# Mixer: the recurrent branch's two gates as products of 64 rows per head

## The chip, the cores and the metric
One Trainium2 chip, one of its cores. The metric is the time of one execution of the whole kernel on the device, in microseconds (us); lower is better. TensorE's clock has two levels, 1.2 and 2.4 GHz, and the trace records which was granted (1.00 is 2.4 GHz, 0.50 is 1.2 GHz).

## The reference
One layer over 2048 positions of width 1024: a mixer of three branches (A: gMLP, B: recurrent, C: S5), an output product, a mixture of experts, a final norm. The change lies in branch B, 6 heads of 64 columns:

```python
xc = causal_depthwise_conv(x_raw, conv_w, conv_b)
xh = xc.reshape(bsz, seq, B_HEADS, HEAD_DIM)
r = sigmoid(einsum("bshi,hij->bshj", xh, rg_w).reshape(bsz, seq, width) + rg_b)
i = sigmoid(einsum("bshi,hij->bshj", xh, ig_w).reshape(bsz, seq, width) + ig_b)
log_a = -LRU_C * r * softplus(-lam)
a = exp(log_a);  b = sqrt(-expm1(2.0 * log_a)) * (i * xc)
h = linear_recurrence(a, b)
return h * gelu(g_raw)
```

Each head has its own 64 x 64 matrix for the gate r and another for the gate i.

## The kernel before, in words
Everything up to the router is in `phases12`. Columns of the mixer lie on partitions: a "column chunk" `i` (0 to 2) of branch B is 128 partitions, two heads of 64. Positions are done in two halves `h` of 1024; a half in two quarters `q` of 512 positions. So `b_z(h, i, w, q)` and the generator `b_post(h, i, q, ...)` run 12 times; each of these runs is called a step here, step 1 to step 12 in the order of the program.

`b_z` issues 2 x 24 products on TensorE (PE) for the two column groups x and g of a chunk (`split3`, L90 to L92, the tile `z`). `b_post` then does: the convolution (ACT L904, DVE L171 on `bxc`), the gelu of g (ACT L914), the two gates (L920 and L921), a chain of ACT operations with two loads of ACT's function tables (L925 to L928), DVE operations and the scan (L934), and the product with the gelu; later its square (ACT L941) and the sums over channels (PE L945).

The gates are the place of the change. For each gate `j` a block-diagonal 128 x 128 matrix `bd[:, j, i, :]` (two heads' 64 x 64 blocks, zeros elsewhere; zeroed once by POOL at L434, filled by four DMAs at L438) is multiplied with `xc`, 128 partitions by 512 positions, and ACT takes the tanh of the product out of PSUM, 128 x 512 at a time, into `btr` (gate r) or `bti` (gate i):

```python
            for j, o in enumerate((tr, ti)):
                ps = bank(psm, "m")
                T.matmul(ps, bd[:, j, i, :], xc, start=True, stop=True)
                A.activation(o, ps, AF.Tanh, scale=0.5, bias=b_cols[:, i, 1 + j:2 + j])
```

In float32 a product is issued to the array as two passes, each with its own load of weights; a step's two products are four passes.

What sets the order: each engine does its instructions in the order in which they were written. The steps, the preparation of the S5 constants (`s5_consts`, `angles`), the S5 batches (`c_batch`), the next weights (`wgen`: ACT L212 and DVE L171 on `w`, which split a weight into a high and a low part) and branch A's later part (`part`) are generators that a ticker (`Flow`) advances between PE's products. A table (`TURNS`) moves some of their turns. The change doesn't touch it, and no generator's turn moves.

PSUM: the products of the gates, the constants' small products (L732), the S5 products (L796 into `u`, L815 to L817 into `y`), the sums (L945) and some transposes (L235) share the pool `psm` of two banks, taken in turn. An instruction that writes a bank waits until the last reader of the use before has read it. So in the kernel before the next user after a step takes the bank of gate r and waits for ACT's first tanh of the step; the one after that takes the bank of gate i and waits for ACT's second.

Of the kernel before, what the change touches and what calls it, by code (L numbers as in the profile page):

```python
# [9 lines left out]
F32 = mybir.dt.float32  # L10
# [3 lines left out]
AF = mybir.ActivationFunctionType  # L14
# [5 lines left out]
P = 128  # L20
# [124 lines left out]
def phases12(tc, io, hd, hc, tab, gcol, ident, c8, stg):  # L145


    nc = tc.nc
    V, A, G, T = nc.vector, nc.scalar, nc.gpsimd, nc.tensor
    ctx = ExitStack()  # L150
    with ctx:
# [4 lines left out]
        base = pool("base")  # L156
# [6 lines left out]
        psm = pool("psm", 2, space=PSUM)  # L163
        drp = pool("dr", space=DRAM)
        yTd = drp.tile([16, P, 8, P], F32, name="yTd")
        bank = lambda p, nm: p.tile([P, 512], F32, name=nm, tag="b")
# [201 lines left out]
        F.add(wg)  # L368

        gv = base.tile([P, 384], F32, name="gv")  # L370
        bd = base.tile([P, 2, 3, P], F32, name="bd")
        wsT = base.tile([P, 6, P], F32, name="wsT")
        glu = base.tile([P, 2, 256], F32, name="glu")
        glb = base.tile([P, 2], F32, name="glb")
# [8 lines left out]
        b_cols = base.tile([P, 3, 4], F32, name="b_cols")  # L383
# [7 lines left out]
        def s5_consts(pp):  # L391
# [39 lines left out]
            yield 0  # L431
            V.memset(hst, 0.0)
            yield 0
            G.memset(bd, 0.0)  # L434
            for j, nm in enumerate(("b_rg_w", "b_ig_w")):
                for h in range(2):
                    src = io[nm][0].rearrange("(i h) a b -> h a i b", h=2)[h]
                    nc.sync.dma_start(out=bd[h * 64:(h + 1) * 64, j, :, h * 64:(h + 1) * 64], in_=src)  # L438
            nc.sync.dma_start(out=gv, in_=io["a_v_norm_g"][0:1, :].to_broadcast((P, 384)))
            yield 0  # L440
            nc.sync.dma_start(out=glu, in_=io["c_glu_w"][0].rearrange("(k p) n -> p k n", p=P))
# [1 line left out]
            ps = bank(pst, "tp")  # L443
# [8 lines left out]
            ps = bank(pst, "tp")  # L452
# [154 lines left out]
            for j in range(2):  # L607
                ps = bank(pst, "tp")
# [88 lines left out]
            for g in range(0, 16, 4):  # L697
                dst = lambda slot: cstP[:, slot, g:g + 4, :]

                i = g // 4 % 2  # L700
# [14 lines left out]
                m = ms[1][:, :, 1:9, :].rearrange("p g s c -> p g (s c)")  # L715
                ps = bank(pst, "tp").rearrange("p (a b) -> p a b", b=P)
                for j in range(4):
                    T.transpose(ps[:, j, :], us[0][:, j].rearrange("p s c -> p (s c)"), ident)
                o = big[2 * i + 1].rearrange("p (a b) -> p a b", b=P)
# [10 lines left out]
                ps = bank(psm, "tp").rearrange("p (a b) -> p a b", b=P)  # L730
# [13 lines left out]
            for h in range(2):  # L744
                ps = bank(pst, "tp").rearrange("p (h j) -> p h j", j=P)
# [153 lines left out]
        def b_post(h, i, q, px, st):  # L899
# [15 lines left out]
            yield  # L915
            tr = bw.tile([P, N], F32, name="btr")
            ti = bw.tile([P, N], F32, name="bti")
            for j, o in enumerate((tr, ti)):
                ps = bank(psm, "m")
                T.matmul(ps, bd[:, j, i, :], xc, start=True, stop=True)  # L920
                A.activation(o, ps, AF.Tanh, scale=0.5, bias=b_cols[:, i, 1 + j:2 + j])  # L921
            yield

            sq = bw.tile([P, N], F32, name="bsq")
# [18 lines left out]
            ps = bank(psm, "m")  # L943
# [1053 lines left out]
```

## Time and profile before

| | us |
|---|---|
| median of 3 runs | 1603.42 (1600.23 to 1604.23) |
| the profiled execution's own time | 1600.41 |
| its span, first to last instruction | 1598.6 |
| mean granted clock | 0.963 |
| PE, ACT, DVE busy | 1492.4, 864.5, 986.4 |
| first product of the gates in steps 1 to 6, at | 99.3, 115.3, 132.8, 154.2, 178.5, 205.8 |
| the same in steps 7 to 12, at | 317.8, 341.5, 355.0, 371.3, 423.9, 448.6 |

The mixer takes about the first 700 us, routing and experts the rest; branch B's steps lie between 99 and 453 us. In the rows below, engines are PE (TensorE's products), PEld (its weight loads), ACT (ScalarE), DVE (VectorE), POOL (GpSimd) and SP (the queue that issues most DMAs). A line such as L921 is a line of the kernel before. A row of a timeline is: start, duration, engine, line, operation, output tile and input tiles, shape, count of merged instructions, and in brackets how long the engine had been idle before and what ended that. Products overlap their neighbours at their ends, so the end of a product in a timeline is later than the moment at which the next one may stream; the chain of waits cuts them to where the next began.

### The profile page before, as it was taken

The page shows a single profiled execution, that of the slowest core. Times are in us where ns is not written, and L with a number is a line of the kernel's source. Part 1 is how long each engine was busy: PE and PEld are TensorE (multiplying, and loading weights), DVE is VectorE, ACT ScalarE, POOL GpSimd, SP SyncE. Part 2 cuts the span into 40 slices and gives each one's busy share as a digit, 9 for nine tenths or more (in the row PEclk, how much of TensorE's full clock was granted, in tenths as well). Part 3 has the DMA queues.
Part 4 walks back from the last instruction along what each step waited for, and adds up shares of the span by engine and source line. Part 5 has one row for each costly group of instructions (what it writes and reads, how often), then busy time and mean ns, then how long its engine had stood idle before and what let it go on. Part 6 is the DMA issues. An engine that isn't in the chain of part 4 may idle for free.

```text
span 1598.6 us, 25576 instructions
## 1 busy us (share of the span) xinstructions
PE 1492.4 (93%) x8373; PEld 1286.7 (80%) x8374; DVE 986.4 (62%) x2011; ACT 864.5 (54%) x1913; POOL 471.1 (29%) x396
## 2 busy tenths in 40 slices
PE   7998879999999999997799899999999999999993
PEld 6866678878899989997588678888888888888882
DVE  6588661674543487887879886668888857303001
ACT  6377543677544534312346546666566665666662
POOL 0132000000000000010355436555555555445442
PEclk9999888999999999998799899999999999999997
DMA  6247632313532726707577887679888877534342
GB/s 179 66 92 139 188 113 76 123 53 105 166 106 73 264 80 233 281 28 265 200 226 233 248 254 202 201 209 278 269 234 230 250 218 209 139 71 111 89 111 77
DMA packets 213774, 267.46 MB, mean 167 GB/s; under 512 B 34824, under 2 KB 178384, under 8 KB 213648
## 3 DMA queue, kind: packets, MB, share of 16 engines
q1 hardware_dynamic: 187808, 201.95, 39.9%
q0 software_dynamic: 24480, 62.27, 16.1%
q10 hardware_dynamic: 1360, 1.57, 0.3%
q8 instruction: 78, 1.28, 0.3%
q14 instruction: 48, 0.39, 0.1%
HBM read 217.09 MB, written 76.94 MB: 184 GB/s over the span
## 4 chain that ended last, share of the span: by engine, by line
PE 74%; DVE 13%; DMA 5%; ACT 4%; issue 2%; SPq 1%; POOL 0%; POOLq 0%; ACTq 0%; DVEq 0%
PE pg L1688 23%; PE z L90 8%; PE z L92 8%; PE z L91 8%; PE pd L1729 4%; PE pd L1728 4%; PE pd L1727 4%; DMA stg<-in_expert_w_up_dram 2%; DVE ring L1614 2%; DVE ring L1596 2%; PE pt L1695 2%; DVE w L171 1%; PE m L920 1%; PE pt L1700 1%; PE ph L1695 1%
## 5 line engine op out<-in xcount | busy, mean ns | idle before, releaser
L1688 PE MATMUL pg<-ring,xs 128*128 x2016 | 487.3, 394 | 11.8 <-DVE ring L1614 10.6
L1688 PEld LDWEIGHTS pg<-ring,xs 128*128 128x128 f32 x2016 | 378.1, 189 | 91.6 <-issue 14.0
L90 PE MATMUL z<-w,xT 128*128 128x256 f32 (+1 forms) x848 | 250.2, 295 | 4.5 <-DVE ht L171 3.2
L92 PE MATMUL z<-w,xT 128*128 128x256 f32 (+1 forms) x848 | 244.3, 288 | 7.2 <-DVE xT L169 7.2
L91 PE MATMUL z<-w,xT 128*128 128x256 f32 (+1 forms) x848 | 244.3, 288 | 0.0
L1596 DVE TENSOR_SCALAR ring<-stg,gcol 128x512 fp32r<-128x512 f32 x242 | 128.5, 592 | 164.8 <-PE pg L1688 86.2
L1614 DVE SCALAR_TENSOR_TENSOR ring<-stg,gcol,ring 128x512 fp32r<-128x512 f32 x248 | 222.2, 956 | 0.0
L92 PEld LDWEIGHTS z<-w,xT 128*128 128x128 f32 x848 | 163.8, 193 | 8.5 <-DVE xT L169 8.5
L90 PEld LDWEIGHTS z<-w,xT 128*128 128x128 f32 x848 | 164.2, 194 | 7.7 <-issue 4.2
L91 PEld LDWEIGHTS z<-w,xT 128*128 128x128 f32 x848 | 164.4, 194 | 1.4 <-issue 1.4
L1727 PE MATMUL pd<-ring,hh 128*128 x336 | 132.1, 393 | 1.7 <-DVE hh L1633 1.7
L1728 PE MATMUL pd<-ring,hh 128*128 x336 | 131.7, 392 | 0.0
L1729 PE MATMUL pd<-ring,hh 128*128 x336 | 131.7, 392 | 0.0
L1892 POOL DMA_INDIRECT hd<-yb,tab x41 | 76.9, 1874 | 182.5 <-ACT yb L1831 182.5
L171 DVE SCALAR_TENSOR_TENSOR w<-raw,vec,w 128x256 fp32r<-128x256 f32 x176 | 82.0, 511 | 61.9 <-ACT w L212 61.8
L1941 POOL TENSOR_TENSOR yb<-yb,gf 128x1024 f32<-128x1024 f32 x40 | 116.9, 2923 | 2.5 <-ACT hu L1856 2.5
L1906 POOL TENSOR_TENSOR hs<-hs,hu 128x256 f32<-128x256 f32 x84 | 99.8, 1188 | 54.4 <-ACT hu L1810 53.7
L90 PE MATMUL z<-xT,w 128*128 128x512 f32 x256 | 110.5, 432 | 0.2 <-ACT xT L298 0.2
L212 ACT ACTIVATE w<-raw,vec 128x256 fp32r<-128x256 f32 x176 | 77.2, 497 | 59.9 <-PE z L92 36.5
L171 DVE SCALAR_TENSOR_TENSOR ht<-z,rsd,ht 128x256 f32<-128x256 f32 x176 | 85.1, 484 | 29.2 <-PE z L92 21.3
L91 PE MATMUL z<-xT,w 128*128 128x512 f32 x256 | 102.2, 399 | 0.2 <-DVE xT L169 0.2
L92 PE MATMUL z<-xT,w 128*128 128x512 f32 x256 | 102.0, 398 | 0.0
(440 smaller groups left out, 2576.7 us busy)
## 6 DMA issues: line engine op xcount, KB each, us to landing
stg<-in_expert_w_gate_dram SPq DMA_DIRECT2D x62, 512.0 KB, 4.3
stg<-in_expert_w_up_dram SPq DMA_DIRECT2D x62, 512.0 KB, 5.8
stg<-in_expert_w_down_dram SPq DMA_DIRECT2D x60, 512.0 KB, 4.5
raw<-in_w_in_dram SPq DMA_DIRECT2D x48, 256.0 KB
raw<-in_w_out_dram SPq DMA_DIRECT2D x24, 512.0 KB
ht<-in_x_dram SPq DMA_DIRECT2D x16, 512.0 KB
yp<-yTd SPq DMA_DIRECT2D x8, 1024.0 KB
hd<-ht SPq DMA_DIRECT2D x16, 512.0 KB
```

Of the source, the lines that this page charges most:

```text
L90: nc.tensor.matmul(ps, ah, bh, start=first, stop=False)
L91: nc.tensor.matmul(ps, ah, bl, start=False, stop=False)
L92: nc.tensor.matmul(ps, al, bh, start=False, stop=last)
L171: stt = lambda o, a, s, b, o0, o1: V.scalar_tensor_tensor(out=o, in0=a, scalar=s, in1=b, op0=o0, op1=o1)
L1596: x = v.tensor_scalar(out=ring[:, r, 0, sl], in0=src[:, sl], scalar1=g, scalar2=None, op0=OP.mult)
L1614: x = v.scalar_tensor_tensor(out=ring[:, r, 1, sl], in0=src[:, sl], scalar=g, in1=hi, op0=OP.mult, op1=OP.subtract)
L1688: i = t.matmul(pg[f], xx[j // 2], w[j % 2], start=k == 0 and j == 0, stop=k == 7 and j == 2)
L1727: t.matmul(pd[n], hh[:, 0, kf], w[0], start=kf == 0, stop=False)
L1728: t.matmul(pd[n], hh[:, 0, kf], w[1], start=False, stop=False)
L1729: i = t.matmul(pd[n], hh[:, 1, kf], w[0], start=False, stop=kf == 3)
L1906: g.tensor_tensor(out=o, in0=o, in1=hu[:, f * 256:(f + 1) * 256], op=OP.mult).then_inc(s_hm, 1)
L1941: g.tensor_tensor(out=z, in0=z, in1=gf, op=OP.mult).then_inc(p_z, 1)
```

## The change
The gates' weights are stored without the zeros: `bd[64h..64h+63, i, :]` holds, for one head, 64 rows and side by side the 64 columns of gate r and the 64 of gate i. A step still has two products, but each is of one head: 64 rows (partitions 0 to 63, or 64 to 127, of `bd` and of `xc`), 128 columns, 512 positions. Its output has gate r of that head on partitions 0 to 63 and gate i on 64 to 127. ACT then takes four tanh of 64 x 512 in place of two of 128 x 512, and each moves its half to the partitions of its head. Both banks are taken before the first tanh.

```diff
@@ -368,7 +368,7 @@
-        bd = base.tile([P, 2, 3, P], F32, name="bd")
+        bd = base.tile([P, 3, P], F32, name="bd")
@@ -431,11 +431,10 @@
-            G.memset(bd, 0.0)
             for j, nm in enumerate(("b_rg_w", "b_ig_w")):
                 for h in range(2):
                     src = io[nm][0].rearrange("(i h) a b -> h a i b", h=2)[h]
-                    nc.sync.dma_start(out=bd[h * 64:(h + 1) * 64, j, :, h * 64:(h + 1) * 64], in_=src)
+                    nc.sync.dma_start(out=bd[h * 64:(h + 1) * 64, :, j * 64:(j + 1) * 64], in_=src)
@@ -915,10 +914,14 @@
             tr = bw.tile([P, N], F32, name="btr")
             ti = bw.tile([P, N], F32, name="bti")
+
+            hv = [slice(0, 64), slice(64, 128)]
+            pp_ = [bank(psm, "m") for _ in range(2)]
+            for r in range(2):
+                T.matmul(pp_[r], bd[hv[r], i, :], xc[hv[r]], start=True, stop=True)
             for j, o in enumerate((tr, ti)):
-                ps = bank(psm, "m")
-                T.matmul(ps, bd[:, j, i, :], xc, start=True, stop=True)
-                A.activation(o, ps, AF.Tanh, scale=0.5, bias=b_cols[:, i, 1 + j:2 + j])
+                for r in range(2):
+                    A.activation(o[hv[r]], pp_[r][hv[j]], AF.Tanh, scale=0.5, bias=b_cols[hv[r], i, 1 + j:2 + j])
             yield
```

Where the instructions stand, on ACT, in step 1, before:

```order
L914 ACT_TABLE_LOAD
L914 ACTIVATE bgg<-z 128x512
L921 ACTIVATE btr<-m,b_cols 128x512 [waits PE_49]
L921 ACTIVATE bti<-m,b_cols 128x512 [waits PE_49]
L925 ACTIVATE bsq<-btr,b_cols 128x512 [waits Activation_49]
L927 ACT_TABLE_LOAD
```

and now (lines of the changed kernel):

```order
L913 ACT_TABLE_LOAD
L913 ACTIVATE bgg<-z 128x512
L924 ACTIVATE btr<-m,b_cols 64x512 [waits PE_49] x2
L924 ACTIVATE bti<-m,b_cols 64x512 x2
L928 ACTIVATE bsq<-btr,b_cols 128x512 [waits Activation_49]
L930 ACT_TABLE_LOAD
```

Nothing else on ACT or DVE has moved; each step has two more ACT instructions in the same place. The tanh of gate r now needs both products, where it needed the first alone. The bank of the step's first product is now read last by ACT's third tanh of four (it was the first of two), that of the second product by the fourth (it was the second).

## Rows read from the trace of the kernel before

**Rows 1.** The page: span and instructions, busy time and share of each engine, and shares of the chain of work that ended last by engine.
```profile
span 1598.6 us, 25576 instructions
PE 1492.4 (93%) x8373; PEld 1286.7 (80%) x8374; DVE 986.4 (62%) x2011; ACT 864.5 (54%) x1913; POOL 471.1 (29%) x396
PE 74%; DVE 13%; DMA 5%; ACT 4%; issue 2%; SPq 1%; POOL 0%; POOLq 0%; ACTq 0%; DVEq 0%
```

**Rows 2.** Busy time by stretch: stretch, its length, each engine's busy time (and instructions), granted clock, share of the DMA engines, GB/s. The engines are, in this order, PE, PEld, DVE, ACT, POOL.
```profile
95.00:165.00 70.00, 57.38 (x252) 41.76 (x251) 55.86 (x108) 57.04 (x94) 17.96 (x15) 0.95 0.78 145
310.00:460.00 150.00, 148.16 (x821) 121.96 (x820) 94.52 (x249) 94.37 (x194) 1.38 (x3) 1.00 0.36 109
```
**Rows 3.** The instructions of the gates by line: count, shortest, median and longest duration in ns, first and last start in us, shapes.
```profile
L920 PE MATMUL m<-bxc,bd x48: 591/592/1223, 99.3 to 449.8; 128*128 128x512 f32 x48
L921 ACT ACTIVATE bti<-m,b_cols x12: 677/688/692, 104.6 to 452.9; 128x512 f32<-128x512 f32 x12
```

**Rows 4.** The chain of waits over the whole run, two of its pieces (start, duration, what): the four passes of a step.
```profile
341.62 1.72 PE m L920 x4
...
424.02 1.82 PE m L920 x4
```

**Rows 5.** Timeline of PE and PEld at two places where the array's tile changes: to and from products of 16 columns (L732, of the constants), and from 128 rows to a transpose of 48 rows (L444), which the built program issues in a tile of 64 rows.
```profile
111.37 0.77 PEld L732 LDWEIGHTS tp<-m,big 128*16 128x16 f32 x8 [0.17 <-issue]
112.35 0.19 PEld L90 LDWEIGHTS z<-xT,w 128*128 128x128 f32 x1 [0.21 <-issue]
...
25.71 0.28 PE L92 MATMUL z<-w,xT 128*128 128x256 f32 x1
...
25.92 0.13 PEld L444 LDWEIGHTS tp<-ident,rows 48*128 48x128 f32 x1
```

**Rows 6.** The chain of waits from 95 to 165 us: start, duration, what.
```profile
104.12 0.58 ACT btr L921
104.69 0.58 ACT bti L921
...
119.77 0.57 ACT btr L921
120.34 0.57 ACT bti L921
...
121.34 0.43 DVE w L171
...
137.33 0.60 DVE kp L733
...
163.74 0.58 ACT btr L921
```

**Rows 7.** Timeline of ACT: its first instruction after the ACT work of step 3 (the copy of the constants' transposes).
```profile
150.42 0.60 ACT L720 ACTIVATE big<-tp 128x512 f32<-128x512 f32 x1 [0.21 <-PE tp L718]
```

**Rows 8.** Timelines of POOL and of DVE around 121 us, behind the tanh of step 2.
```profile
120.53 1.64 POOL L169 TENSOR_TENSOR big<-big 128x512 f32<-128x512 f32 x1 [10.44 <-DVE big L688]
...
125.19 1.22 POOL L688 TENSOR_TENSOR m<-pw,big 128x576 f32<-128x576 f32 x1
...
123.95 2.75 DVE L170 TENSOR_SCALAR an<-an 128x520 f32<-128x520 f32 x1
```

**Rows 9.** Timeline of PE: its two longest waits between 95 and 310 us.
```profile
137.97 2.08 PE L920 MATMUL m<-bxc,bd 128*128 128x512 f32 x2 [4.05 <-DVE kp L733]
...
164.37 1.87 PE L945 MATMUL m<-ones,bxc 128*128 128x1 f32 x8 [5.57 <-ACT btr L921]
```

**Rows 10.** Timeline of ACT from step 8 to step 10, and in step 12. From the first row to that at 374.69 us it shows one idle time, that of the second row.
```profile
343.37 0.69 ACT L921 ACTIVATE bti<-m,b_cols 128x512 f32<-128x512 f32 x1
...
356.69 0.69 ACT L921 ACTIVATE btr<-m,b_cols 128x512 f32<-128x512 f32 x1 [0.47 <-DVE bxc L934]
...
374.69 0.68 ACT L921 ACTIVATE btr<-m,b_cols 128x512 f32<-128x512 f32 x1
...
376.44 1.09 ACT L238 ACTIVATE raw<-tp 128x512 f32<-128x512 f32 x2 [0.49 <-PE tp L235]
...
452.34 0.69 ACT L921 ACTIVATE btr<-m,b_cols 128x512 f32<-128x512 f32 x1 [2.54 <-DVE bxc L934]
```

**Rows 11.** Timeline of PE: the next users of the bank of gate r after steps 9, 10 and 12. None of them waited.
```profile
359.49 1.88 PE L992 MATMUL m<-uv,wsT 128*128 128x512 f32 x4
...
375.81 1.03 PE L235 MATMUL tp<-ident,raw 128*128 128x128 f32 x8
...
453.11 0.45 PE L815 MATMUL m<-cpm,cx 128*128 128x128 f32 x2
```

**Rows 12.** By line, as in Rows 3: one DVE copy of few partitions, one ACT operation of one partition, and two ACT copies out of PSUM of 128 partitions.
```profile
L733 DVE COPY kp<-tp x4: 671/676/679, 100.8 to 151.9; 16x512 f32<-16x512 f32 x4
L1313 ACT ACTIVATE tab<-tp x1: 262/262/262, 765.4 to 765.4; 1x144 int32<-1x144 f32 x1
L791 ACT ACTIVATE cx<-tp x16: 365/383/385, 174.9 to 455.8; 128x256 f32<-128x256 f32 x16
L852 ACT ACTIVATE yc<-tp x8: 579/596/619, 250.6 to 482.8; 128x512 f32<-128x512 f32 x8
```

**Rows 13.** Busy time by stretch, as in Rows 2: what follows PE's wait that ended at 164.37 us.
```profile
164.40:172.00 7.60, 7.60 (x22) 6.34 (x23) 2.49 (x6) 7.54 (x12) 0.00 (x0) 0.50 0.85 241
```

**Rows 14.** Timeline of PEld at the start: the first weight load that needs loaded data.
```profile
6.08 0.18 PEld L343 LDWEIGHTS vps<-ident,rows 8*128 8x128 f32 x1 [0.33 <-DMA rows<-in_norm_mix_g_dram]
```

## The prediction
> **What bounds the kernel now.** I read the page first, for the engine that sets the end: PE is busy 93% of the span and makes 74% of the chain that ended last, ACT 4% [rows 1]. A reader might stop there and count PE alone. But a share is a mean over stages, so the table by stretches comes next. In 310 to 460 us PE is busy 148.16 of 150 us; in 95 to 165 us, where steps 1 to 4 lie, it is busy 57.38 of 70, as much as ACT with 57.04 and DVE with 55.86 [rows 2]. So there are two regimes: steps 7 to 12 where PE hardly stops, and steps 1 to 4 where the chain decides. The chain from 95 to 165 us runs through ACT, then DVE, and comes back to PE at a copy (L733) at 137.33; it passes the four tanh of steps 1 and 2 and the first of step 4 [rows 6]. PE's two long waits there are 4.05 us for that copy, and 5.57 us for ACT's first tanh of step 4, whose bank the sums (L945) take over [rows 9]. The two lines of the change are small: 48 passes, and 12 tanh for each of the two gates [rows 3]. What they cost depends on where ACT or PE has room.
>
> **The prices.** *Products.* The chain gives a step's four passes 1.72 us, 0.43 each [rows 4]. After the change there are still two products of two passes. If nothing overlaps, the passes cost the same 1.72; if the two products, which use different rows of the array, run wholly side by side, 0.86. No row shows two products side by side, so these are the bounds. I take three pass times, 1.29: instructions issue in the order written, so the second product's first pass can at best stand beside the first one's second. To this come two changes of the array's tile. Where the trace has such changes, weight loads of other products follow on without a gap, but here they start 0.17 and 0.21 us late; before the 64-row transpose the load starts 0.21 us after the start of the product ahead, and not under it [rows 5]. I take 0.2 us for each change. So a step costs PE between 0.86 + 0.4 - 1.72 = -0.46 and 1.72 + 0.4 - 1.72 = +0.4 us, and I take 1.29 + 0.4 - 1.72 = -0.03, which is nothing.
>
> On that overlap, the Trainium skill, TensorE: Matmul & The Clock Gate, Part 3 (packing small matmuls), says that products on different row groups run at the same time and start some 4 ns apart. That would be the lower bound, -0.46 a step, and the forecast below would lose 0.43 us in steps 6 and 11, 0.9 in all; no run here shows it yet.
>
> *Tanh.* Two of 128 x 512 become four of 64 x 512. In the chain one costs 0.57 to 0.58 us [rows 6]. If the price went with partitions, halves would cost half and nothing were added. The rows speak against it: two ACT copies out of PSUM take 383 and 596 ns for 256 and 512 elements, 0.83 ns for each element more; carried down to 144 elements that is 383 - 112 x 0.83 = 290 ns, and the one ACT row of a single partition has 262 ns at 144 elements. DVE takes 676 ns for 512 elements of 16 partitions [rows 12]. So each of the four costs what one did: 2 x 0.575 = +1.15 us per step on ACT (bounds 0 and 1.15), 13.8 us in all, and the bank of the first product comes free after the third tanh instead of the first, also +1.15.
>
> *No price.* POOL's memset of the zeros is gone, but the start waits for a DMA, not for POOL [rows 14]; the four weight DMAs move the same bytes.
>
> **What of it lies on the path, step by step.**
> - Step 1: its tanh are on the chain, DVE behind them waits for ACT: +1.15.
> - Step 2: its tanh are on the chain too (119.77, 120.34, then DVE at 121.34). But DVE is then held up: POOL works without a gap from 120.53 to 126.41, a DVE operation started at 123.95 takes 2.75 us and ends with POOL [rows 8]. POOL starts from DVE's work before the tanh, so it moves by step 1's 1.15 alone. I take +0 (bounds 0 and 1.15). PE's wait ending at 137.97 so moves by 1.15.
> - Step 3: ACT works on until 150.42, where it had been idle for 0.21 us [rows 7]. The copy there starts the last DMAs of the constants, for which ACT waits before step 4. 1.15 - 0.21 = +0.94.
> - Step 4: the sums wait for the step's first bank [rows 9]; now for the third tanh: +1.15. Together 3.24 us by 164 us.
> - Step 5: ACT has room; the second product waited for DVE before, so no overlap: only the change back, +0.2. Step 6: 0. Step 7: its second product waits for DVE, +0.2. Step 11: 0.
> - Steps 8 to 10: from 343.37 to 374.69 ACT has one idle time, 0.47 us, and that one waits for DVE, which itself follows ACT's operations of step 8 [rows 10]. So the extra of steps 8 and 9 adds up on ACT, 2.3 us. Behind step 10 the transposes (L235) at 375.81 take the first bank [rows 11]; before, the tanh that freed it began at 374.69 and took 0.57, so 375.26, 0.55 us ahead. Now: 374.69 + 2.3 + 3 x 0.575 - 375.81 = 2.9 us late. Step 8 can start its second tanh somewhat earlier if the products overlap (0.2), so I take +2.7.
> - Step 12: the first tanh starts at 452.34 after DVE [rows 10], the third would end at 454.07; L815 took its bank at 453.11 [rows 11]: +1.0.
>
> Sum: 3.24 + 0.4 + 2.7 + 1.0 = **+7.3 us**. What follows the mixer starts from its end, and I see no wait on anything that is not moved with it. The profiled execution took 1600.41 us, so it would be 1607.7; it stands 3.0 under the median of 1603.42. Put on the median, which is what will be compared, the forecast is **1610.7 us**.
>
> **The rivals.**
> - *The extra tanh are mostly hidden* (no change). If steps 1 and 4 keep their delay but steps 3 and 8 to 12 find room, 2.3 + 0.4 = 2.7 us is left: 1606.1. For it: ACT is busy 94.37 of 150 us in 310 to 460 [rows 2], so it has time in the mean, and one of its idle times waits for DVE. Against: no idle time over 0.5 us between 343 and 375 [rows 10].
> - *The products side by side* (faster). PE sets the pace everywhere, ACT's lateness disappears in waits that exist anyway, and the two products run together: 12 x -0.46 = -5.5 us, 1597.9. It decides from the point at which an overlap saves more than the two changes of tile, 0.4 us a step, and only if the tanh of halves cost less than I take. For it: 93% PE. Against: rows 6, 9 and 12. The rule of the Trainium skill named above (TensorE: Matmul & The Clock Gate, Part 3) would lead here if PE alone counted.
> - *The slow clock* (much slower). After PE's wait to 164.37 it was granted 0.50 for 7.6 us [rows 13], a loss of 3.8 us. If one of the longer waits, or the new one before L235, brings another such stretch: 1610.7 + 3.8 = 1614.5.
> - *No overlap, only changes of tile*: +0.43 in steps 6 and 11 above the forecast; where ACT sets the pace it is hidden in ACT's lateness: 1611.6, inside the forecast.
>
> **Numbers.** About 0.3% (4.8 us) is what a measurement of this kernel can tell from no change; the runs before spread over 4.0 us. I give the forecast 0.53, the hidden tanh 0.27, the slow clock 0.13, the side-by-side products 0.07. The range of the first three, with the bounds of step 2 (+1.15) and of the spread of runs, is 1602 to 1617; the faster rival is left out. Faster than 1598.6: 0.07. Within 1598.6 to 1608.2: 0.27. Slower: 0.53 + 0.13 = 0.66.
>
> **What would show it.** Right: tanh of 64 x 512 at about 0.68 us each in their row; ACT busy about 14 us more; the wait of the sums of step 4 longer by some 2 us, a new wait of 2 to 3 us before L235 behind step 10, and about 1 us before L815 behind step 12; the passes of a step's two products either 0.43 us apart (no overlap) or starting in pairs. Wrong: halves at 0.35 to 0.45 us (the whole sum falls to nearly nothing), no wait before L235, or PE's time from 310 to 460 us shrinking because the products run side by side.

## The result, and the profile of the changed kernel

The change is slower: median 1619.98 us of 4 runs (1615.42 to 1624.97) against 1601.95 before (1600.23 to 1604.23), a ratio of 1.0112 (95% interval 1.0087 to 1.0138), or +18.0 us. The forecast was +7.3, with a range up to 1617. The direction came out; the size was more than twice the forecast's. The profiled execution of the change took 1618.09 us, 17.7 more than that of before.

The page of the changed kernel (span, busy time, chain by engine) answers [rows 1]:

```profile
span 1616.4 us, 25608 instructions
PE 1504.5 (93%) x8373; PEld 1292.0 (80%) x8374; DVE 977.7 (60%) x2011; ACT 885.3 (55%) x1937; POOL 472.0 (29%) x395
PE 69%; DVE 13%; ACT 8%; DMA 5%; issue 2%; SPq 1%; POOL 0%; ACTq 0%; POOLq 0%; DVEq 0%
```

ACT has 20.8 us more work, where 13.8 were forecast, and 8% of the chain where it had 4%. Busy time by stretch, as in [rows 2]:

```profile
95.00:165.00 70.00, 60.13 (x246) 42.63 (x244) 54.28 (x107) 60.05 (x96) 16.48 (x15) 0.92 0.72 133
310.00:460.00 150.00, 142.60 (x738) 114.21 (x736) 86.95 (x234) 102.58 (x202) 1.21 (x3) 0.98 0.34 104
```

From 310 to 460 us PE was busy 148.16 us and is now 142.60, and its clock, 1.00 before, is 0.98. So PE stands idle for 7.40 of these 150 us, where it was 1.84. ACT is busy 8 us longer. By line, as in [rows 3]:

```profile
L921 PE MATMUL m<-bxc,bd x48: 589/664/1217, 99.1 to 466.6; 64*128 64x512 f32 x48
...
L924 ACT ACTIVATE btr<-m,b_cols x24: 667/680/685, 103.7 to 470.8; 64x512 f32<-64x512 f32 x24
L924 ACT ACTIVATE bti<-m,b_cols x24: 682/686/689, 105.2 to 472.2; 64x512 f32<-64x512 f32 x24
```

A tanh of 64 x 512 lasts what one of 128 x 512 did, as forecast. How often one can start is another matter. ACT's timeline in step 1 of the change (start, duration, engine, line, ..., merged count):

```profile
103.75 1.38 ACT L924 ACTIVATE btr<-m,b_cols 64x512 f32<-64x512 f32 x2
105.15 1.40 ACT L924 ACTIVATE bti<-m,b_cols 64x512 f32<-64x512 f32 x2
106.57 0.82 ACT L928 ACTIVATE bsq<-btr,b_cols 128x512 f32<-128x512 f32 x1
```

From the first tanh to L928 it is 2.82 us for four: 0.70 each. The same place in the kernel before:

```profile
104.01 0.68 ACT L921 ACTIVATE btr<-m,b_cols 128x512 f32<-128x512 f32 x1
104.58 0.69 ACT L921 ACTIVATE bti<-m,b_cols 128x512 f32<-128x512 f32 x1
105.15 0.82 ACT L925 ACTIVATE bsq<-btr,b_cols 128x512 f32<-128x512 f32 x1
```

There two took 1.14 us, 0.57 each as in the chain [rows 6], since a tanh of 128 x 512, 0.68 us long, let the next one start 0.11 us before its end. The halves do not. So a step adds 2.82 - 1.14 = 1.68 us to ACT and not 1.15.

What PE waited for from 95 to 480 us (engine, tile, line, releaser: us in total, times, longest):

```profile
PE m L948 <- ACT bti L924: 8.2, 1, 8.2
...
PE tp L235 <- ACT bti L924: 2.9, 1, 2.9
...
PE m L814 <- ACT bti L924: 2.0, 1, 2.0
...
PE m L995 <- ACT bti L924: 0.8, 1, 0.8
```

The first three are the places that the forecast named: the sums of step 4 [rows 9], L235 behind step 10 and the S5 product behind step 12 [rows 11]. They have the new releaser, a tanh of the second pair. The fourth, of L995 behind step 9, was not forecast. Now PE's timeline: the products of step 1 and those of step 10, and the wait of L235.

```profile
99.08 1.12 PE L921 MATMUL m<-bxc,bd 64*128 64x512 f32 x2
101.25 1.12 PE L921 MATMUL m<-bxc,bd 64*128 64x512 f32 x2 [1.05 <-DVE kp L732]
...
383.04 1.13 PE L921 MATMUL m<-bxc,bd 64*128 64x512 f32 x4 [0.65 <-ACT junk L1013]
384.10 0.50 PE L90 MATMUL z<-xT,w 128*128 128x512 f32 x1
...
390.10 1.97 PE L235 MATMUL tp<-ident,raw 128*128 128x128 f32 x8 [2.94 <-ACT bti L924]
```

Where both banks are free (step 10; so too in steps 8, 9 and 12, and with 1.17 us in step 4) the four passes take 1.06 us and not 1.72: the two heads' products run side by side. Where the second bank comes late (step 1), each product takes its own 1.06. Finally the clock behind the wait (stretch, length, PE's busy time, granted clock, DMA share, GB/s), in the change:

```profile
386.00:388.00 2.00, 1.16 (x5) 1.00 0.00 0
388.00:390.00 2.00, 0.00 (x0) 0.96 0.85 252
390.00:392.00 2.00, 1.90 (x10) 0.50 0.94 222
392.00:394.00 2.00, 2.00 (x10) 0.50 0.60 181
394.00:396.00 2.00, 2.00 (x6) 0.50 0.00 0
396.00:398.00 2.00, 2.00 (x10) 0.83 0.00 0
```

After the wait PE works at half its clock, 1.2 GHz, until about 396.7 us. Before there was no slow stretch between 310 and 460 us [rows 2].

**Lag.** To place the loss I compare the start of the same PE instruction in two traces: trace of a variant minus trace of the kernel before. All that the change loses, it loses in branch B's steps: its lag is 19.2 us at 480 us and 17.7 at the end.

| lag in us at (time in the trace before) | 165 | 178 | 187 | 215 | 310 | 372 | 385 | 480 |
|---|---|---|---|---|---|---|---|---|
| change | 4.2 | 3.6 | 6.3 | 9.4 | 9.5 | 11.4 | 17.4 | 19.2 |
| change, second profile (e9) | 3.8 | 3.5 | 5.9 | 6.3 | 6.5 | 8.4 | 14.5 | 15.7 |
| 128 rows, four tanh (e1) | 5.0 | 4.9 | 5.4 | 7.1 | 7.6 | 9.6 | 15.3 | 16.9 |
| 64x64 tiles, two tanh (e5) | 1.1 | 0.8 | 1.3 | 3.1 | 3.6 | 5.1 | 4.8 | 5.9 |
| extra ACT work alone (e6) | 2.1 | 1.2 | 3.4 | 3.5 | 3.6 | 4.6 | 5.8 | 6.3 |
| halves in place (e8) | 2.8 | 2.3 | 5.5 | 7.2 | 4.7 | 6.6 | 9.0 | 9.1 |
| change, wait filled (e10) | 5.3 | 5.0 | 7.4 | 7.7 | 7.9 | 9.7 | 12.7 | 14.4 |
| before, one late bank (e12) | 0.3 | -0.9 | 0.3 | 3.2 | 0.7 | 0.8 | 7.9 | 7.8 |
| before, bank less late (e18) | 0.4 | -0.7 | 0.4 | 3.3 | 0.9 | 0.8 | 2.7 | 2.5 |
| before, branch C's wait filled (e17) | 2.4 | 1.4 | 2.4 | 5.4 | 3.1 | 3.1 | 3.1 | 2.9 |

The last three run the code of the kernel before up to step 10 (e12, e18) or up to 266 us (e17). What they lag until there, up to 2.4 us at 165 and 5.4 at 215, is the difference between profiles of one code.

### The profile page after: what moved, and what is told of

Read it like the earlier page. It is cut to its first block, busy times and chain, and to the rows that moved or that the text cites. A ratio compares the mean times of both kernels' runs of the same rounds, so it can differ in the third digit from the quotient of the medians.

```text
span 1616.4 us, 25608 instructions
## 1 busy us (share of the span) xinstructions
PE 1504.5 (93%) x8373; PEld 1292.0 (80%) x8374; DVE 977.7 (60%) x2011; ACT 885.3 (55%) x1937; POOL 472.0 (29%) x395
## 4 chain that ended last, share of the span: by engine, by line
PE 69%; DVE 13%; ACT 8%; DMA 5%; issue 2%; SPq 1%; POOL 0%; ACTq 0%; POOLq 0%; DVEq 0%
PE pg L1691 23%; PE z L90 8%; PE z L92 7%; PE z L91 7%; PE pd L1731 4%; PE pd L1730 4%; PE pd L1732 4%; DMA stg<-in_expert_w_up_dram 2%; DVE ring L1617 2%; DVE ring L1599 2%; PE pt L1698 2%; DVE w L171 1%; PE pt L1703 1%; PE ph L1698 1%; DVE ht L171 1%
## 5 line engine op out<-in xcount | busy, mean ns | idle before, releaser
L1691 PEld LDWEIGHTS pg<-ring,xs 128*128 128x128 f32 x2016 | 378.5, 190 | 89.1 <-issue 11.4
L1599 DVE TENSOR_SCALAR ring<-stg,gcol 128x512 fp32r<-128x512 f32 x242 | 133.1, 610 | 169.1 <-PE pg L1691 86.1
L1617 DVE SCALAR_TENSOR_TENSOR ring<-stg,gcol,ring 128x512 fp32r<-128x512 f32 x248 | 209.7, 905 | 0.0
L90 PE MATMUL z<-xT,w 128*128 128x512 f32 x256 | 109.9, 429 | 0.2 <-ACT xT L298 0.2
L91 PE MATMUL z<-xT,w 128*128 128x512 f32 x256 | 104.7, 409 | 0.2 <-DVE xT L169 0.2
L92 PE MATMUL z<-xT,w 128*128 128x512 f32 x256 | 104.0, 406 | 0.0
```

What stands on the lines that cost most here:

```text
L90: nc.tensor.matmul(ps, ah, bh, start=first, stop=False)
L91: nc.tensor.matmul(ps, ah, bl, start=False, stop=False)
L92: nc.tensor.matmul(ps, al, bh, start=False, stop=last)
L1599: x = v.tensor_scalar(out=ring[:, r, 0, sl], in0=src[:, sl], scalar1=g, scalar2=None, op0=OP.mult)
L1617: x = v.scalar_tensor_tensor(out=ring[:, r, 1, sl], in0=src[:, sl], scalar=g, in1=hi, op0=OP.mult, op1=OP.subtract)
L1691: i = t.matmul(pg[f], xx[j // 2], w[j % 2], start=k == 0 and j == 0, stop=k == 7 and j == 2)
```

## The experiments

Each was compared with the kernel before on the same chip. "Lost to the clock" is span x (1 - mean granted clock), the mean over a kernel's runs.

| variant | us more than before (medians) | ratio, 95% interval | lost to the clock |
|---|---|---|---|
| before (23 runs; 58.8 to 60.5 beside the other variants) | | | 59.3 |
| change | 18.0 | 1.0112 (1.0087, 1.0138) | 72.0 |
| e9, change again | 19.1 | 1.0120 (1.0100, 1.0141) | 71.2 |
| e1, 128 rows, four tanh | 16.7 | 1.0100 (1.0074, 1.0125) | 66.5 |
| e3, tanh by head | 19.4 | 1.0125 (1.0098, 1.0151) | 72.0 |
| e5, 64x64 tiles, two tanh | 4.4 | 1.0031 (1.0021, 1.0041) | 62.0 |
| e6, extra ACT work | 4.9 | 1.0029 (1.0015, 1.0043) | 59.5 |
| e7, L235 on other banks | 13.5 | 1.0098 (1.0077, 1.0119) | 67.2 |
| e8, halves in place | 11.7 | 1.0082 (1.0063, 1.0101) | 63.1 |
| e10, change, wait filled | 14.5 | 1.0099 (1.0078, 1.0120) | 66.7 |
| e11, e1, wait filled | 12.6 | 1.0082 (1.0062, 1.0102) | 63.9 |
| e12, before, one late bank | 6.5 | 1.0049 (1.0031, 1.0067) | 64.1 |
| e18, before, bank less late | 3.0 | 1.0013 (0.9996, 1.0029) | 59.6 |
| e13, before, two waits filled | 5.1 | 1.0043 (1.0026, 1.0059) | 57.6 |
| e15, before, more filled | 2.9 | 1.0029 (1.0013, 1.0045) | 55.4 |
| e14, change, three filled | 17.8 | 1.0114 (1.0096, 1.0133) | 64.4 |
| e16, change, more filled | 16.6 | 1.0100 (1.0083, 1.0116) | 58.9 |
| e17, before, branch C's filled | -2.2 | 0.9992 (0.9975, 1.0008) | 57.7 |

The change loses 12 to 13 us more to the clock. My first theory was that products of 64 rows bring that; the rival, that ACT's four tanh do.

### Products or tanh: e1 to e4

e1: the change with zeros for the other head, so that each product uses 128 rows.

```diff
-                T.matmul(pp_[r], bd[hv[r], i, :], xc[hv[r]], start=True, stop=True)
+                T.matmul(pp_[r], bd[:, r, i, :], xc, start=True, stop=True)
```

> The changed kernel, but each head's product runs over all 128 rows, with zeros in the other head's 64: four tanh of 64x512 as in the change, and the products take no part of the array only. Theory A (products of 64 rows make the clock fall: between 95 and 480 us the clock was granted 0.50 for 34.1 us before and 58.0 us after, 11.9 us of work lost more): the slow stretches go back to about 34 us, and what is left are the tanh: +6 to +8 us against the kernel before (about 1609). Theory B (ACT's longer work stretches PE's waits, and these make the clock fall): slow stretches stay near 58 us, +16 to +20 us (about 1620). Theory C (chance: where the slow stretches fall is moved about by any delay): between the two, with other places.

Measured: +16.7. Nearly all of the change's loss is there without any product of 64 rows, so theory A falls. Clock loss is 66.5, between the two.

e2: the change's products, but two tanh of 128 x 512.

```diff
-                for r in range(2):
-                    A.activation(o[hv[r]], pp_[r][hv[j]], AF.Tanh, scale=0.5, bias=b_cols[hv[r], i, 1 + j:2 + j])
+                A.activation(o, pp_[j], AF.Tanh, scale=0.5, bias=b_cols[:, i, 1 + j:2 + j])
```

> The changed kernel's products of 64 rows, but two tanh of 128x512, one for each bank, straight to btr and bti (half of each then holds the other gate, so the values are not the reference's). ACT's work and the release of the banks are as in the kernel before. Theory A (64 rows make the clock fall): slow stretches between 95 and 480 us stay near 55 us; +10 us from the clock, less about 0.64 us in each step in which the two products run side by side and PE sets the pace (some 6 steps, 4 us): +5 to +10 us. Theory B (ACT's waits make the clock fall): slow stretches as before, no tanh extra, the overlap is won: -4 us, between -6 and 0.

Its values differ, and from the routing on (about 700 us) the time is then not that of the same work; so only the mixer counts. Its lag at 640 us is 4.2 us, which neither case forecast, and 3.8 of that were there at 235 us. The old code itself lags 3.0 to 5.4 us there (e12, e17, e18), so no loss can be laid to the products. The test with the reference's values is e5.

e3: the four tanh by head.

```diff
-            for j, o in enumerate((tr, ti)):
-                for r in range(2):
+            for r in range(2):
+                for j, o in enumerate((tr, ti)):
```

> The changed kernel with the four tanh in the order of the banks: both gates of the first head, then both of the second. The first bank comes free after the second tanh and not the third, btr is complete one tanh later. If the release of the first bank is what PE waits for (sums of step 4, L235 behind step 10, L814 behind step 12), each of these waits gets 0.58 us shorter and the whole 1.5 to 2 us shorter than the change: about +16 us against the kernel before. If the clock is decided by the length of these waits (theory B), the stretch behind step 10 may go as well: +12. If ACT's total sets it, no difference to the change: +18.

+19.4, as the change; lag 5.6 from 372 to 385 us where the change has 6.0. The wait of L235 was 2.2 us instead of 2.9, but the slow clock behind it stayed. So the order brought no gain that shows; 1.5 to 2 us could not be told within this interval (+15.7 to +24.2 us).

e4: the kernel before with the product of gate r alone.

```diff
+                if j == 0:
                     ps = bank(psm, "m")
                     T.matmul(ps, bd[:, j, i, :], xc, start=True, stop=True)
```

> The kernel before with the product of gate r alone; both tanh read its bank (gate i's product is left out). 128 rows, half of the passes: PE has less work in each step, as in the change where two products run side by side. Theory A (rows of the product decide): no more slow stretches than before (34 us), 0.86 us less in the steps in which PE sets the pace, -3 to -8 us. If it is the smaller time of PE's work in the step that lets the clock fall: slow stretches above 50 us and +3 us or more.

Again only the mixer counts: lag -7.8 us at 640 us. That is inside the first case (-3 to -8): PE's smaller work alone brings no loss.

### One part at a time: e5, e6, e8

e5: one gate of one head is a product of its own, and ACT takes two tanh of 128 x 512 (as e2's `+` line).

```diff
-            for r in range(2):
-                T.matmul(pp_[r], bd[hv[r], i, :], xc[hv[r]], start=True, stop=True)
+            for j in range(2):
+                for r in range(2):
+                    T.matmul(pp_[j][hv[r]], bd[hv[r], i, hv[j]], xc[hv[r]], start=True, stop=True)
```

> The product of one gate of one head is a tile of its own, 64 rows by 64 columns, two of them side by side on opposite corners of the array; a bank holds one gate of both heads, and ACT takes two tanh of 128x512 as in the kernel before. All values are the reference's. If products on a part of the array make the clock fall: more slow time than the kernel before (its runs lose span x (1 - clock) = about 59.5 us), and +5 us or more. If only ACT's tanh matter: four pass pairs of 0.53 us are 2.1 us a step where four passes took 1.72, so +0.4 us in the six steps where PE sets the pace and +0 to +3 us in all, slow time 58 to 62 us.

+4.4 is between the two cases, and 62.0 lost to the clock is the top of the lower one. Products on a part of the array don't make the clock fall much.

e6: two more tanh on ACT, with the banks released as before.

```diff
+            for r in range(2):
+                A.activation(sq[r * 64:r * 64 + 64], tr[r * 64:r * 64 + 64], AF.Tanh, scale=0.5)
```

> The kernel before with two more tanh of 64x512 on ACT in each step, from btr into bsq (which the next instruction overwrites), behind the two tanh of the gates: ACT has the change's extra work, but both banks and bti are released as before. If the banks' later release is what costs, PE's waits for L921 stay as they are and the whole is +2 to +5 us. If it is ACT's lateness as such (everything ACT does after it), +10 us or more, and a wait of over 1 us before L235 behind step 10 from step 8's and 9's extra alone (2 x 1.4 us less 0.55).

+4.9 and no more lost to the clock. L235 now waited 0.9 us, where the second case wanted over 1. So ACT's lateness by itself costs about 5 us, the upper end of the first case (the two extra tanh took 1.30 us a step, where the change adds 1.68); what the change loses beyond that needs the later banks and the later `bti`, or the clock.

e8: the kernel before, each tanh cut in two.

```diff
+                for hh in (slice(0, 64), slice(64, 128)):
+                    A.activation(o[hh], ps[hh], AF.Tanh, scale=0.5, bias=b_cols[hh, i, 1 + j:2 + j])
```

> The kernel before with each tanh cut into two of 64x512 that stay on their partitions (read and written at the same ones): no product changes. In the change a tanh of 64x512 starts 0.70 us after the one before it, a 128x512 one 0.57, so four take 1.68 us more than two and not 1.15. If halves as such cost 0.70: 1.4 to 1.7 us more per step and +13 to +18 us in all, near the variant with 128 rows and four tanh (+16.7). If the move to other partitions is the price: 0.57 each, 1.15 more per step, and +7 to +11 us.

+11.7. ACT's timeline in its step 1:

```profile
103.33 1.37 ACT L922 ACTIVATE btr<-m,b_cols 64x512 f32<-64x512 f32 x2
104.73 1.38 ACT L922 ACTIVATE bti<-m,b_cols 64x512 f32<-64x512 f32 x2
106.14 0.82 ACT L926 ACTIVATE bsq<-btr,b_cols 128x512 f32<-128x512 f32 x1
```

2.81 us for four: the price of halves is the change's, without any move to other partitions. The total is lower than I took from that price (13 to 18), and this difference led to the clock: e8 has the same ACT work as e1, and 5 us less.

### The wait behind step 10: e7, e10, e11, e12, e18

e7: L235's first transposes on the other pool's banks.

```diff
-                ps = bank(pst if kk else psm, "tp").rearrange("p (k n) -> p k n", n=P)
+                ps = bank(pst, "tp").rearrange("p (k n) -> p k n", n=P)
```

> The changed kernel with the first transposes of L235 in the other pool of banks (the two of the transposes), so that they don't take the first bank of the gates. Behind step 10 the change waited 2.9 us there and the clock was then granted 0.50 for 6.8 us (3.4 us of work). If that wait brings the slow stretch: both go, 6 us less than the change, about +12 against the kernel before. If the sums behind it (L948, the next user of the bank) wait in its place, or the slow stretch comes by chance: +16 to +19.

+13.5, but by the trace the wait only moved: the sums (L948) now wait 2.1 us there, and the slow stretch is behind them. What made the difference in the median I can't say.

e10: the change, with three products in the wait that the transposes then overwrite.

```diff
+            if k == 3:
+                for _ in range(3):
+                    T.matmul(banks[1], ident, raw[:, 4:8, :], start=True, stop=True)
```

> The changed kernel, and in the turn behind step 10 PE does three products of 128x512 (six passes of 0.43 us, 2.6 us) into the bank of the second transposes, which then overwrite them, before the first transpose that waits 2.9 us for the gates' bank. The wait is as long, but PE is busy in it. If PE's idleness there is what brings the clock of 0.50 for 6.8 us behind it: no slow stretch there, and 3.4 us less than the change itself. If the slow stretch has another cause (64 rows, chance): the same as the change, or up to 0.5 us more.

14.5 instead of 19.1 us beside it. PE's timeline, and the clock, in e10 (the first row are the fills):

```profile
385.31 2.74 PE L235 MATMUL tp<-raw,ident 128*128 128x512 f32 x6
388.41 1.09 PE L239 MATMUL tp<-ident,raw 128*128 128x128 f32 x8 [0.36 <-ACT bti L928]
```

```profile
386.00:388.00 2.00, 2.00 (x5) 1.00 0.72 208
388.00:390.00 2.00, 1.64 (x16) 1.00 0.92 219
390.00:392.00 2.00, 2.00 (x11) 1.00 0.76 229
```

The bank comes no sooner, yet the slow stretch is gone; the lag from 372 to 385 us is 3.0 and not 6.0. So PE's idleness brought it, and not the products of 64 rows, which e10 has too.

e11: the same fill in e1.

> The variant with products over 128 rows and four tanh, with the same three products put into its wait behind step 10. It was +16.7 us, and its slow stretch behind step 10 also 6.8 us. If the idle wait brings it: +13 us, as the variant with halves in place (+11.7), which had a shorter wait and no slow stretch there. If not: +16 to +17.

+12.6, as forecast; lag from 372 to 385 us 2.6 instead of 5.7.

e12: the kernel before, one bank late in one step.

```diff
+                for _ in range(7 if (j, h, i, q) == (0, 1, 1, 1) else 1):
```

> The kernel before, but in step 10 alone the first tanh is done seven times (the same values each time): its bank is released 6 x 0.57 = 3.4 us later, 2.9 us behind the moment at which L235 wants it; before, it was free 0.55 us ahead. Nothing else differs. If one such wait costs itself and a slow stretch of the clock behind it: 2.9 + 3.4 = +6.3 us. If only itself: +2.9. If it is taken up later: 0.

+6.5. The repeats started 0.72 us apart (each records a wait for ACT's own semaphore, which the one before it updates), so the wait was 3.8 us and not 2.9:

```profile
380.51 1.16 PE L235 MATMUL tp<-ident,raw 128*128 128x128 f32 x8 [3.78 <-ACT btr L922]
```

```profile
378.00:380.00 2.00, 0.00 (x0) 1.00 0.97 240
380.00:382.00 2.00, 1.49 (x12) 0.85 0.31 92
382.00:384.00 2.00, 2.00 (x8) 0.50 0.00 0
...
386.00:388.00 2.00, 2.00 (x6) 0.50 0.00 0
388.00:390.00 2.00, 2.00 (x19) 0.94 0.00 0
```

e18: the same with four tanh instead of seven.

> The kernel before, with the first tanh of step 10 done four times instead of seven: in the longer variant the repeats started 0.72 us apart and the wait of L235 was 3.8 us, so now 3 x 0.72 - 0.55 = 1.6 us. If a wait of that length brings the slow stretch as well: 1.6 + 3.4 = +5 us. If not (the variant with halves in place waited 1.6 us there and had none): +1.6 us.

+3.0 by the medians (interval -0.6 to +4.6); in the trace, which until step 10 runs like e12's:

```profile
378.43 1.09 PE L235 MATMUL tp<-ident,raw 128*128 128x128 f32 x8 [1.61 <-ACT btr L922]
```

```profile
378.00:380.00 2.00, 1.57 (x15) 1.00 0.97 238
380.00:382.00 2.00, 2.00 (x11) 1.00 0.35 104
382.00:384.00 2.00, 2.00 (x16) 1.00 0.00 0
```

A wait of 1.6 us cost 1.8 us of lag; one of 3.8 cost 7.2, 3.4 more than itself. e8 too waited 1.6 us here and had no slow stretch, where e1 with 2.3 us had one. This is shown from both sides: taking the idleness away removes the stretch, adding it to the kernel before brings it. That holds for this wait. Elsewhere the length of a wait alone does not tell: in step 1 of the change PE waited 1.05 us, and the clock of 0.50 followed at 103.1 us; in step 1 of the kernel before it waited 1.22 us, and the clock stayed at 1.00.

### The rest of the clock's loss: e9, e13 to e17

e9: the change once more.

> The changed kernel once more, for another profile and more times beside the variants of this round. If the slow stretches of the clock behind steps 1, 2 and 5 come from the change (its products of 64 rows), they are in this profile too, between 95 and 480 us about 58 us of 0.50. If they come by chance (where PE's short waits happen to fall), they are in other places and their sum differs: 44 to 62 us. The stretch behind step 10, after the wait of L235, is there in both cases. +17 to +20 us against the kernel before.

+19.1, and 51 us of 0.50 between 95 and 480 us. The stretches behind steps 2, 5 and 10 were there again, that behind step 1 was not, and that in step 6 came earlier and was shorter. So neither case came whole. In e7, which is the same kernel up to step 10, those behind steps 2 and 5 are missing too. Busy time and clock around step 5 in the change (first fence) and in e7 (second):

```profile
180.00:190.00 10.00, 8.84 (x33) 0.83 0.55 163
```

```profile
180.00:190.00 10.00, 9.34 (x46) 1.00 0.50 151
```

Lag from 178 to 187 us: 2.7 us with the slow stretch, 0.7 without it (4.6 to 5.3 in e7).

e13 and e15: the kernel before with products that nobody reads in its own waits; e14 and e16: the change with the same ones.

```diff
+        def fill(n):
+            if not n:
+                return
+            two = [bank(pst, "tp") for _ in range(2)]
+            for m in range(2 * n):
+                T.matmul(two[m % 2][:, 0:192], ident, bd[:, 0].rearrange("p a b -> p (a b)")[:, 0:192], start=True, stop=True)
...
+            fill({(0, 1, 0): 7, (0, 2, 0): 7}.get((h, i, q), 0))
             ps = bank(psm, "m")
```

This is e13. In e15 and e16 `fill` stands also between the two products of the gates (1, 1 and 4 in steps 1 to 3; in e16 also 1 in step 5) and before L877; e14 and e16 have e10's fill too.

> The kernel before, with products of 128x192 that nobody reads put into the two longest waits of PE: before the sums of step 3 (5.57 us at 164.37 us, filled with 14 products, about 4.5 us) and of step 5 (5.35 us at 230.08). If an idle wait is what brings the slow stretch of the clock that follows each (0.50 to 172.0 us, a loss of 3.8 us, and to 236.8 us, a loss of 3.4 us): 7 us less than before, about 1594, faster than both kernels. If the slow stretches are independent of the waits, or other work is slowed by the products: 0 to +2 us.

> The changed kernel with the same two waits filled (the first, 8.2 us, with 20 products) and the one behind step 10 as in the earlier variant. If idle waits bring the slow stretches: 3.8 + 3.4 + 4.4 = 11 to 12 us less than the change, +7 us against the kernel before, and 14 to 15 more than the kernel before with its two waits filled. If not: as the change, +18.

> The kernel before with its shorter waits filled as well: between the two products of the gates in steps 1 to 3 (1.2, 1.1 and 4.05 us) and before the sums of branch C at 266.58 us (1.7 us; a slow stretch to 277 us follows). If idle waits bring the slow stretches: another 3 to 6 us less than with two filled, and hardly a slow stretch between 95 and 300 us. If short waits don't matter: as with two filled.

> The changed kernel with all these waits filled. If idle waits are the whole of the clock's part: hardly a slow stretch between 95 and 400 us, and 6 to 8 us more than the kernel before with all filled (the plain lateness: 3.2 us by step 4, 2.7 to 3 behind step 10, 1 to 2 behind step 12). If the products of 64 rows make the clock fall by themselves: slow stretches stay behind steps 1, 2, 5 or 6, where the kernel before with all filled has none, and the difference stays at 12 us or more.

In all four the gain forecast for the filled waits did not come: e13 +5.1, e15 +2.9, e14 +17.8, e16 +16.6. The other cases fit the numbers of e14 (+18), e15 (2.2 us from e13) and e16 (13.7 above e15), but not of e13 (0 to +2). PE's timeline in e13 tells why (L904 are the fills):

```profile
158.55 4.71 PE L904 MATMUL tp<-bd,ident 128*128 128x192 f32 x28
163.46 1.05 PE L953 MATMUL m<-ones,bxc 128*128 128x1 f32 x8 [0.20 <-ACT btr L928]
...
179.04 1.19 PE L927 MATMUL m<-bxc,bd 128*128 128x512 f32 x1 [3.92 <-DVE cv L169]
...
232.55 6.48 PE L904 MATMUL tp<-bd,ident 128*128 128x192 f32 x26 [5.36 <-DVE gtmp L169]
```

The first fill did its work: the slow stretch from 162 us is gone, and PE was 4.4 us ahead at 175. There it had to wait 3.92 us for DVE: DVE and ACT set the pace, and the gain was given back, the rest of it to a new slow stretch (a clock of 0.79 from 176 to 184 us). The second fill took a bank that was itself not free, waited as long as the sums had, and then stood in their way for 6.5 us. So these four don't separate the sizes. But e16 shows one thing (stretches as above):

```profile
95.00:165.00 70.00, 66.74 (x301) 1.00 0.72 134
165.00:183.00 18.00, 15.41 (x79) 1.00 0.72 198
183.00:190.00 7.00, 5.53 (x10) 0.55 0.77 232
```

Up to 183 us it has no slow stretch at all, and at 165 us it lags by 3.9 us, as the change does with 4.2. e15, also without one up to 165 us, lags by 0.0 there. So in steps 1 to 4 the change costs about 4 us without the clock, and the clock adds nothing that shows.

e16's other case named a rival: products of 64 rows leave slow stretches in steps 5 and 6 where e15 has none. They are there (the last row above, and 0.86 from 204 to 216 us; e15 has 1.00 from 180 to 190 and from 204 to 216). But e8, whose products all have 128 rows, has them as well:

```profile
180.00:190.00 10.00, 8.08 (x34) 0.83 0.62 187
204.00:216.00 12.00, 7.94 (x41) 0.86 0.49 154
```

So they don't need products of 64 rows. What brings them is open.

e17: a fill in branch C's wait alone, before the sums L877.

```diff
+            fill(2 if h == 0 else 0)
             ps = bank(psm, "m")
```

> The kernel before, with four products of 128x192 that nobody reads (1.3 us) in the 1.7 us that PE waits before the sums of branch C at 266.58 us, and no other fill. In the kernel before the clock was 0.50 for 10 us behind that wait. If PE's idleness brings that stretch: shorter or gone, 3 to 4 us less than before, faster than both kernels. If it comes from elsewhere (a second wait of 0.88 us stays): 0, and up to 1 us more.

-2.2 us with an interval from -4.0 to +1.3: no difference shown. Its stretch behind that wait lasted 6.8 us, but so it does in e12 and e18, which have no fill there. No variant with the reference's values beats the kernel before.

## Why the prediction was wrong, step by step

Two steps failed. A tanh of half the partitions was priced at 0.575 us and costs 0.70, and the sum puts at nothing what TensorE's clock does behind the new wait, which cost 3 us. About 3 us more stay without a shown cause.

- **The passes: right in kind, undersized.** Four passes side by side take 1.06 us; I took 1.29 and thought of 0.86 as the end. In e2's steps 8 to 10, where ACT's work is as before, each step takes 0.46 us off the lag (from 4.5 us to 3.1 in three steps): my lower bound, not the -0.03 that I took. The order of issue, my reason against it, does not hold the second product back: in step 10 the two first passes start 0.007 us apart. The Trainium skill, TensorE: Matmul & The Clock Gate, Part 3 (packing small matmuls), says that products on different row groups run at the same time; the trace agrees (step 10: four passes in 1.06 us). In the change PE loses this again where it next waits for ACT, for instance 0.8 us at L995 behind step 9.
- **The tanh: the term that was mis-sized.** "Each of the four costs what one did" holds for the duration, 0.68 us. But I priced it at 0.575, the distance of starts in the chain [rows 6], which contains an overlap of 0.11 us with the neighbour, and carried that overlap over to the halves. Halves, in place or moved, start 0.70 apart. It is +1.68 a step, not +1.15.
- **Steps 1 to 4**: forecast 3.24. With 1.68 in place of 1.15 in step 1, 1.68 - 0.21 in step 3, and a first bank that is free 1.40 us later in step 4 (the third tanh ends at 2 x 0.70 + 0.68, the first did at 0.68), the same sum gives 4.6. Four profiles of this code gave 4.2, 3.8, 4.7 (e7) and 5.3 (e10). The extra of step 2, which I took to be hidden by POOL, isn't needed for this. But the old code itself lags 0.3 to 2.4 us there (e12, e17, e18), so the agreement is no better than 2 us.
- **Steps 5 to 7**: forecast +0.4, two changes of tile. In step 7 the lag of the change grows by 0.2 us, as forecast; in step 5 it can't be told apart. The lag at 310 us was 9.5, 6.5, 7.5 and 7.9 in these profiles: 3 us more on average than 4.6 + 0.4. Slow stretches that come in some profiles and not in others are there. Three profiles with the old steps up to 266 us (e12, e17, e18) have one too, between 200 and 213 us, and lag 3.2, 5.4 and 3.3 at 215, but 0.7, 3.1 and 0.9 at 310, where branch C's stretch is shorter. So the profile of the kernel before, with a clock of 1.00 from 204 to 216 us, is the odd one, and a part of the 3 us can be its luck. Whether the change makes such stretches more frequent is open. [rows 9] are also not the two longest waits up to 310 us: PE waited 5.35 us before the sums of step 5, at 230.08, and the forecast left that wait out. It hardly changed (5.4 us at L948).
- **Steps 8 to 10**: the chain of waits held. With the right price, 374.69 + 2 x 1.68 + 2.1 - 375.81 = 4.3 us; with the wait filled, the lag grew by 4.8 from 310 to 385 us (e10), by 4.6 in e11. The forecast said +2.7. On top come 3 us: the slow clock behind the wait, 7.9 in all.
- **Step 12**: forecast +1.0, corrected 452.34 + 2.1 - 453.11 = 1.3; measured 1.8 (change) and 1.3 (e9), from 385 to 480 us.
- **The slow clock**: the rival with a chance of 0.13 is what happened, and at the very wait that I had forecast, though its 1614.5 us is 5.5 short. Its price of 3.8 us was about right (3.0 to 3.4 measured); its chance was not. I had a row in which a slow stretch followed an idle PE [rows 13] and set a new idle time of nearly 3 us on PE's path without asking this of it. The Trainium skill, TensorE: Matmul & The Clock Gate, Part 1 (the HAM clock gate), says that the gate follows how busy PE has been; e10, e12 and e18 agree (a clock of 1.00 behind the filled wait, 0.50 behind one of 3.8 us, 1.00 behind one of 1.6).

The account: 4.6 + 0.4 + 4.3 + 1.3 = 10.6 us from the tanh (0.4 of it the changes of tile), 3 from the clock behind step 10, about 3 in steps 5 to 7 with the clock of 0.50 in most profiles; 16.6 against 17.7 between the two profiled executions. The last 3 are placed, not explained. Of the 12 to 13 us more that the change loses to the clock, this puts 6 on the path; what became of the others is not shown. With the waits filled in both kernels, e16 loses 3.5 us more to the clock than e15 and is 13.7 us slower. As an estimate that leaves 10.2 us for the tanh, near the 10.6.

## What to carry to other kernels

Price an instruction that is cut in two by the distance between starts of the pieces, not by the distance that the whole one has in a chain: that one may include an overlap which the pieces lose. When a change puts a new wait on TensorE's path, add the clock behind it to the price: before the transposes L235 a wait of 1.6 us cost itself and one of 2.2 to 3.8 cost about 3 us more. Filling an idle wait keeps its gain only where TensorE sets the pace behind it, and only if the fill itself waits for nothing.

## What the runs showed of the chip that I had not expected

- ACT operations of 64 x 512 don't overlap their successor: tanh out of PSUM start 0.70 us apart with 0.68 of duration, from SBUF 0.64 with 0.63 (e6); 128 x 512 ones start 0.57 apart with 0.68. The two halves of `bti` record no wait for each other, so it is not the program that holds them apart; why is open. The seven tanh of 128 x 512 in e12 also started 0.72 apart, but there each records a wait for the one before.
- Two float32 products of 64 rows side by side: pairs of passes 0.53 us apart, where single passes of 128 rows followed at 0.43. It isn't the running side by side that costs: a lone product of 64 rows has 0.53 too (step 1: 1.06 for two passes). In e5 a step has four pairs; they took 1.86 us in step 8 (the next product started at 347.19), and the inner ones followed at 0.43:

```profile
345.33 1.93 PE L922 MATMUL m<-bxc,bd 64*64 64x512 f32 x8
```

- Traces of one kernel differ by up to 3 us of lag (change and e9 at 310 us), and what differs in them is where the slow stretches fall. So a single profile can't settle 2 us here.
